# An encoder layer whose residual stream is kept as rows of tokens instead of rows of channels

## The chip, the cores and the metric

The kernel runs on one core of one Trainium2 chip. The metric is the device time of one launch in microseconds (us); the profiled execution is read beside it. Engines are named as in the profile: PE (TensorE, the matrix engine; PEld its loads of the stationary operand), DVE (VectorE), ACT (ScalarE), POOL (GpSimd) and SP (SyncE, which issues nearly all DMAs here, in order).

## The reference, cut to what matters

Two sequences (`x_prompt`, s = 0, and `x_sample`, s = 1) of 512 tokens of 1024 channels go through one layer:

```
x = x + 0.5 * swiglu(rms_norm(x, ffn1_norm), ...)          # 2816 hidden channels
h = rms_norm(x, mix_norm)
proj = h @ w_in        # queries, keys, values of attention and of the memory, gates
merged = sigmoid(g_att) * (att @ w_up_att) + sigmoid(g_mlstm) * (mem @ w_up_mlstm)
x = x + merged @ w_out
x = x + 0.5 * swiglu(rms_norm(x, ffn2_norm), ...)
y = rms_norm(x, final_norm)

def rms_norm(x, g): return x * rsqrt(mean(x * x, axis=-1) + EPS) * g
def swiglu(x, w_gate, w_up, w_down): return (silu(x @ w_gate) * (x @ w_up)) @ w_down
```

All is float32; every matrix product is made as three matmuls of high and low parts (hi x hi, hi x lo, lo x hi).

## The kernel before, in words

PE multiplies along the partitions (128 rows of the on-chip memory), so activations that enter a product as the contracted operand must have channels on the partitions. The kernel keeps the residual stream that way all along: `xbuf[s]` and `x2buf[s]` in DRAM are `[128, 8, 512]`, eight blocks of 128 channels by 512 tokens.

Stages, in order of the program:

- **Start.** `load_x` brings both inputs as token rows. For s = 0, `turn` (L1176) transposes each 128 x 128 block on PE; `keep_x` (L1181) copies the eight results out of PSUM on ACT and stores them to `xbuf[0]`. `norm_x` (DVE L1191, then the row scale, then the scaling on DVE L1199 and ACT L1197, in place) normalizes the token rows, and `turn` transposes them for ffn1 (L1218).
- **ffn1 up** (`Up.begin` for seven blocks, whose results are kept in DRAM, then `Up.rest`, a loop over 22 blocks of the hidden channels, products at L301, side work such as DVE L330 and ACT L310). The two sequences are combined in a scheme of seven products (B11, B21, B22, T4, T1, T2_, T3) instead of eight. `late_x`, called in eight rounds of the loop, transposes s = 1's input on PE (L1266) and stores it to `xbuf[1]`.
- **ffn1 down** (`ffn_down`): 28 steps, seven products for each of four chunks of hidden blocks. `products` (L545) holds weights as the stationary operand and streams 512 tokens, so PSUM gets channels by tokens. `flush_` (L562) adds half of it to the residual `xs[s]`, which was loaded from `xbuf` in four loads of 1 MB. In the last seven steps each finished 128-channel block goes to `done`: `done1` stores it, splits s = 0's for the mixer (`emit_hl`, L144 and L145), and sums squares (`sq_add`: ACT L155, POOL L156). In ffn2 the last step is done in two halves of 256 tokens.
- **The norm's scale.** A sum over channels is a sum over partitions here: `stats` transposes the sum of squares (PE L188, DVE L190), computes 1/rms (`rstd_cols`, 12 small DVE instructions, L166 to L177), and `bcast_cols` spreads it over the partitions (PE L198, DVE L204) as `R[s]`.
- **Mixer** (`mix(s, ...)`, once per sequence). It multiplies inputs that carry the gain but not yet 1/rms. The results that have tokens on the partitions (`tok_proj`, PE L695) are scaled by `r[s]` in ACT's eviction (L769 to L774); the ones with channels on the partitions (`win_cols`, PE L711) by a product with `R[s]` on DVE (L867, L876, L991, L1034). The last part works `mem_gate` and `merge_mem` for eight blocks (L1034, L1041, L1042, split into `mh`, `ml` at L613 and L614), and calls `prep1` or `prep2` for each, which prepare the next stage's input of the other sequence. Then `out_unit`, eight times, multiplies with `w_out` (PE L711, DVE L1144) into channels by tokens.
- **ffn2**, like ffn1; its begin reloads s = 1 from `x2buf[1]` and scales it (`normed`, L609).
- **Final norm.** `done2` collects the blocks; `turn_out` (L1363) transposes all of it back to token rows, 64 transposes, and `put_out` (ACT L1369, POOL L1370, DVE L1372) scales and stores.

The order of work is the program's, moved by a scheduler with priorities (`shifted`, `pin`). On chip there are seven slots of 16 KB per partition (`A(...)`: inputs, mixer tensors, residuals), four raw and four split weight buffers, and eight PSUM banks in four kinds (MM three, PO one, PS two, PT two).

Of the kernel before, what the change touches and what calls it, by code (L numbers as in the profile page):

```python
# [16 lines left out]
P = 128  # L17
# [9 lines left out]
def encoder(ctx, tc, I, outs):  # L27
# [121 lines left out]
    def sq_add(src, acc, tag="t2", qtag="f2"):  # L149
        if acc is None:  # L150
            acc = T2(F32, tag)
            nc.scalar.activation(acc, src, AF.Square)
            return acc
        q = T2(F32, qtag)
        nc.scalar.activation(q, src, AF.Square)  # L155
        nc.gpsimd.tensor_tensor(acc, acc, q, op=ALU.add)  # L156
        return acc

    def rstd_cols(v, width, n):


        def t_(dt=F32):
            return spool.tile([P, width], dt, tag=f"rs{width}", bufs=5, name=nm("rs"))
# [17 lines left out]
    def stats(acc):  # L181

        return rstd_cols(col_sums(acc), 4, D)

# [15 lines left out]

    def bcast_cols(r):
        pr = bcast_psum(r)
        R = T2(F32, "R")
        nc.vector.tensor_copy(R, pr)  # L204
        return R

# [182 lines left out]
    class Up:  # L389
# [23 lines left out]
        def rest(self, raw, late=None, at=None, hook=None):  # L413
# [12 lines left out]
            for i, j in enumerate(ORDER):  # L426
                W = left
                nxt = ORDER[i + 1] if i + 1 < NF else None
                turn_late = late(i, ring) if late else None
# [10 lines left out]
                if turn_late:  # L440
                    turn_late()
# [19 lines left out]
    def ffn_down(wd, rb, ring, tail, xres, done, at_step, hook, halves=None):  # L461
# [71 lines left out]
        def products(i, ts, ds=range(DH)):  # L533
# [3 lines left out]
            for d in ds:  # L537
                if first:
                    banks[grp, d] = (((PS, PS, PT, PT) if grp == "Y" else (MM, MM, MM, PO))[d])()
                p = banks[grp, d][:, ts]  # L540
                us = left[i]
                for q, u in enumerate(us):
                    r = right[(i + 3) % 4][q]
                    for k, (a, b) in enumerate(((0, 0), (0, 1), (1, 0))):
                        nc.tensor.matmul(p, u[:, a, d * P:(d + 1) * P], r[:, b, ts],  # L545
                                         start=(first and q == 0 and k == 0), stop=(q == len(us) - 1 and k == 2),
                                         skip_group_check=True)
                flush_(i, d, p, ts)
# [4 lines left out]
        def flush_(i, d, p, ts):  # L553
# [7 lines left out]
            else:  # L561
                V_.scalar_tensor_tensor(acc[:, ts], p, 0.5, acc[:, ts], op0=ALU.mult, op1=ALU.add)  # L562
# [8 lines left out]
            elif m == B21:  # L571
                add(xs[1][:, DH + d], e5[:, d])
                done(0, d, None)
            elif m == T4:
                done(0, DH + d, None)
            elif m == T1:
                done(1, DH + d, None)
            elif m == B22 and ts.stop - ts.start == S:
                done(1, d, None)
            elif m == B22 and d == DH - 1:  # L580
                done(1, d, ts.start * 2 // S)
# [6 lines left out]
        whole = slice(0, S)  # L588
        for s, h in ((0, 0), (1, 1), (0, 1), (1, 0)):
            nc.sync.dma_start(xs[s][:, h * DH:(h + 1) * DH, :], xres[s][:, h * DH:(h + 1) * DH, :])  # L590
        sums(CHUNKS[0])
        tail()
        for i in range(n):
            if i == n - 1 and halves:
                products(i, slice(0, S // 2))
                products(i, slice(S // 2, S))
            else:
                products(i, whole)
# [7 lines left out]

    def normed(xt, g, R, d):

        V_.scalar_tensor_tensor(xt, xt, g[:, d:d + 1], R, op0=ALU.mult, op1=ALU.mult)  # L609
# [104 lines left out]
    def mix(s, xh, xl, early=None, extra=None, after=None):  # L714
# [52 lines left out]
        def kv_done(pk):  # L767
            for b in range(4):
                nc.scalar.activation(kraw3[:, b, :], pk[b][:, 0:P], AF.Copy, scale=r[s][:, b:b + 1])  # L769
                nc.scalar.activation(Gt[:, b * 16:(b + 1) * 16], pk[b][:, 2 * P:2 * P + 16], AF.Copy,  # L770
                                     scale=r[s][:, b:b + 1])
                pv = pk[b][:, P:2 * P].rearrange("p (k e) -> p k e", k=HK)
                nc.scalar.activation(Vst[:, b, :, 0:DA], pv, AF.Copy, scale=r[s][:, b:b + 1])
                V_.scalar_tensor_tensor(Vst[:, b, :, DA:2 * DA], pv, r[s][:, b:b + 1], f(Vst[:, b, :, 0:DA]),  # L774
                                        op0=ALU.mult, op1=ALU.subtract)
# [11 lines left out]
        def q_done(pq):  # L787
            ssq = small(32, "ssq")
            for b in range(4):
                t = T2()  # L790
                nc.scalar.activation(t, pq[b], AF.Copy, scale=r[s][:, b:b + 1])
# [58 lines left out]
        def mem_values():  # L850
            def done(pvv):
                vm = A([P, 2, 4, S], F32R, "Vm")
                for b in range(4):
                    nc.scalar.activation(vm[:, 0, b, :], pvv[b], AF.Copy, scale=r[s][:, b:b + 1])
                    V_.scalar_tensor_tensor(vm[:, 1, b, :], pvv[b], r[s][:, b:b + 1], f(vm[:, 0, b, :]),
                                            op0=ALU.mult, op1=ALU.subtract)
# [16 lines left out]
        def out_gate(h):  # L873
            def done(pp):
                og = T2(F32, "ac")
                V_.tensor_tensor(og, pp, R[s], op=ALU.mult)  # L876
                nc.scalar.activation(og, og, AF.Tanh, scale=0.5)
# [16 lines left out]
        if early:  # L894
            early()
        go(*tok_proj(xh, xl, [(0, 512)], 2, q_done), mem_qk(0, 0))
        yield None
        gates()
# [99 lines left out]
        for h in range(HA):  # L998
# [5 lines left out]
            if h == 2 and extra:  # L1004
                extra()
# [25 lines left out]
        def mem_gate(d):  # L1031
            def done(pp):
                t = ths[d] = T2()
                V_.tensor_tensor(t, pp, R[s], op=ALU.mult)  # L1034
                nc.scalar.activation(t, t, AF.Tanh, scale=0.5)
# [426 lines left out]
```

## Time and profile before

| what | value |
|---|---|
| time, median of 3 runs | 2139.46 us (2139.08 to 2140.02) |
| profiled execution, span | 2143.1 us |
| PE busy | 2084.7 us (97%) |
| DVE busy | 1633.9 us (76%) |
| ACT busy | 957.6 us (45%) |
| POOL busy | 145.4 us (7%) |
| DMA | 370.23 MB, mean 173 GB/s |

The span is that of one profiled execution; its own time is the span, 3.6 us above the median of the runs. In a line of the profile, `L545 PE MATMUL pst<-rt,w 128*128 128x512 f32 x18` is a group of 18 matmuls of line 545 into a PSUM tile `pst` from `rt` and `w`, 512 columns wide; behind it, in brackets, stands how long the engine was idle ahead of it and what released it. A row of the windows gives, for a stretch from A to B: its length, the busy time and the instruction count of PE, PEld, DVE, ACT and POOL, the clock granted to PE (1.00 is full), the busy share of the DMA engines and GB/s. A row of the waits gives an engine's instruction, what it waited for, the sum of waiting, how often and the mean. A row of groups gives busy time and mean ns, then the idle time ahead and what ended it. A row of DMA issues gives the KB of each and the us from issue to landing.

### The profile page before, as it was taken

How to read it: one execution, taken by the hardware profiler on the slowest of the kernel's cores; microseconds unless marked ns; L12 is line 12 of the kernel's file. 1: busy time of each engine (PE TensorE's matmuls, PEld its weight loads, DVE VectorE, ACT ScalarE, POOL GpSimd, SP SyncE). 2: the span in 40 equal slices, each digit the busy share in tenths (PEclk: the TensorE clock that was granted, in tenths of full speed). 3: DMA queues.
4: the chain of work that ended last, by engine and by line, in shares of the span. 5: the costliest groups of instructions: out<-in, count | busy, mean ns of one | idle time of the engine just before them, and what ended most of it. 6: DMA issues, size and time to landing. Idle time of an engine off the chain costs nothing.

```text
span 2143.1 us, 27234 instructions
## 1 busy us (share of the span) xinstructions
PE 2084.7 (97%) x9544; PEld 1699.1 (79%) x9544; DVE 1633.9 (76%) x2895; ACT 957.6 (45%) x1693; POOL 145.4 (7%) x138
## 2 busy tenths in 40 slices
PE   7999999999999999999999999999999999999997
PEld 6878788887888777878887777877778788888886
DVE  7888887875797798675659967665878887776795
ACT  6534444442234456463436664434434444443222
POOL 0000000001002011100121011011000000000002
PEclk9999999999999999999999999999999999999999
DMA  9566654489765222342352233347465554389752
GB/s 293 164 206 194 214 198 151 147 305 371 275 221 164 64 76 67 92 116 73 115 167 69 69 91 104 110 148 215 153 197 172 190 190 151 123 301 384 272 190 105
DMA packets 314776, 370.23 MB, mean 173 GB/s; under 512 B 18608, under 2 KB 209088, under 8 KB 313616
## 3 DMA queue, kind: packets, MB, share of 16 engines
q1 hardware_dynamic: 314048, 367.23, 52.2%
q0 software_dynamic: 592, 1.27, 0.3%
q8 instruction: 75, 1.23, 0.2%
q14 instruction: 61, 0.50, 0.1%
HBM read 259.35 MB, written 109.08 MB: 172 GB/s over the span
## 4 chain that ended last, share of the span: by engine, by line
PE 79%; DVE 10%; DMA 6%; ACT 3%; issue 2%; SPq 0%; POOL 0%; DVEq 0%; ACTq 0%; POOLq 0%
PE mm L711 17%; PE pss L301 14%; PE pst L301 8%; PE mm L545 8%; PE mm L301 8%; PE pss L545 4%; PE pst L545 4%; PE mm L695 4%; PE pso L545 3%; DMA wr<-in_ffn_w_up_dram 2%; DMA rbuf<-t 1%; PE pso L974 1%; PE pso L695 1%; PE pst L967 1%; PE pss L948 1%
## 5 line engine op out<-in xcount | busy, mean ns | idle before, releaser
L711 PE MATMUL mm<-xh,w 128*128 128x512 f32 x896 | 290.6, 395 | 0.0
L301 PE MATMUL pss<-xc,w 128*128 128x512 f32 x1056 | 258.6, 392 | 9.2 <-DVE t L330 9.2
L301 PE MATMUL mm<-xc,w 128*128 128x512 f32 x1056 | 259.0, 394 | 5.5 <-ACT f L310 4.1
L301 PE MATMUL pst<-xc,w 128*128 128x512 f32 x1056 | 255.4, 390 | 0.0
L301 PEld LDWEIGHTS pss<-xc,w 128*128 128x128 f32 x1056 | 196.5, 188 | 56.1 <-DVE t L330 15.7
L301 PEld LDWEIGHTS mm<-xc,w 128*128 128x128 f32 x1056 | 197.6, 189 | 51.2 <-ACT f L310 7.8
L301 PEld LDWEIGHTS pst<-xc,w 128*128 128x128 f32 x1056 | 197.3, 188 | 43.2 <-ACT t L334 2.5
L711 PEld LDWEIGHTS mm<-xh,w 128*128 128x128 f32 x896 | 167.0, 188 | 32.5
L221 ACT ACTIVATE w<-wr 128x1024 fp32r<-128x1024 f32 (+1 forms) x112 | 114.6, 1029 | 166.7 <-issue 61.0
L545 PE MATMUL mm<-rt,w 128*128 128x512 f32 (+1 forms) x819 | 186.3, 383 | 1.7 <-DMA rt<-rbuf 1.7
L711 PE MATMUL mm<-xl,w 128*128 128x512 f32 x448 | 176.5, 394 | 0.0
L545 PEld LDWEIGHTS mm<-rt,w 128*128 128x128 f32 x819 | 150.2, 188 | 32.2 <-DMA rt<-rbuf 1.9
L222 DVE TENSOR_TENSOR w<-wr,w 128x1024 fp32r<-128x1024 f32 (+1 forms) x112 | 140.4, 1254 | 42.5 <-ACT w L221 41.1
L259 ACT ACTIVATE w<-t 128x512 fp32r<-128x512 f32 x176 | 107.2, 628 | 126.5 <-DVE t L285 46.8
L260 DVE TENSOR_TENSOR w<-t,w 128x512 fp32r<-128x512 f32 x176 | 118.3, 688 | 40.4 <-ACT w L259 37.4
L301 PE MATMUL pss<-xc,f 128*128 128x512 f32 x528 | 128.7, 392 | 0.2 <-DVE t L338 0.2
L301 PEld LDWEIGHTS pss<-xc,f 128*128 128x128 f32 x528 | 98.1, 188 | 24.1 <-DVE t L338 4.1
L613 ACT ACTIVATE w<-wr 128x512 fp32r<-128x512 f32 x72 | 44.7, 631 | 131.6 <-PE pso L545 63.4
L613 ACT ACTIVATE w<-t 128x512 fp32r<-128x512 f32 x82 | 51.8, 632 | 112.6 <-PE pst L545 51.6
L711 PEld LDWEIGHTS mm<-xl,w 128*128 128x128 f32 x448 | 84.2, 188 | 16.1
L545 PE MATMUL pss<-rt,w 128*128 128x512 f32 x396 | 94.3, 389 | 0.2 <-DMA rt<-rbuf 0.2
L545 PE MATMUL pst<-rt,w 128*128 128x512 f32 x396 | 93.7, 389 | 0.0
(328 smaller groups left out, 3746.2 us busy)
## 6 DMA issues: line engine op xcount, KB each, us to landing
rt<-rbuf SPq DMA_DIRECT2D x154, 512.0 KB, 5.6
wr<-in_w_in_dram SPq DMA_DIRECT2D x72, 512.0 KB, 3.9
wr<-in_ffn_w_gate_dram SPq DMA_DIRECT2D x56, 512.0 KB, 5.4
rbuf<-tab SPq DMA_DIRECT2D x90, 256.0 KB, 3.6
wr<-in_ffn_w_up_dram SPq DMA_DIRECT2D x44, 512.0 KB, 4.4
rbuf<-t SPq DMA_DIRECT2D x88, 256.0 KB, 3.6
rbuf<-f SPq DMA_DIRECT2D x66, 256.0 KB, 3.5
rbuf<-R SPq DMA_DIRECT2D x64, 256.0 KB, 3.8
```

The costliest lines, as they stand in the source:

```text
L221: pin(nc.scalar.activation(hi, raw, AF.Copy))
L222: pin(lo_eng.tensor_tensor(lo, raw, f(hi), op=ALU.subtract))
L259: pin(nc.scalar.activation(t[:, 0], src, AF.Copy))
L260: pin(V_.tensor_tensor(t[:, 1], src, f(t[:, 0]), op=ALU.subtract))
L301: nc.tensor.matmul(p, a[:, k, :], xt[:, b, k, :], start=(first and k == 0 and i == 0), stop=(k == HK_ - 1 and i == 2), skip_group_check=True)
L545: nc.tensor.matmul(p, u[:, a, d * P:(d + 1) * P], r[:, b, ts], start=(first and q == 0 and k == 0), stop=(q == len(us) - 1 and k == 2), sk ...
L613: nc.scalar.activation(hi, src, AF.Copy)
L695: nc.tensor.matmul(p[b][:, :N], a[:, k, bs], w_[:, kl, :], start=(k == 0 and i == 0), stop=(k == KD - 1 and i == 2))
L711: nc.tensor.matmul(p, a[:, k, :], b, start=(k == 0 and i == 0), stop=(k == n - 1 and i == 2))
L948: nc.tensor.matmul(p, qT[:, h, b * P:(b + 1) * P], kv[:, hk * 2 + j, :], start=(j == 0), stop=(j == 1))
L967: nc.tensor.transpose(p[:, b * P:(b + 1) * P], Ps[b][:, kb * P:(kb + 1) * P], ident)
L974: nc.tensor.matmul(po, Vst[:, kv_, hk, :], w, start=(kv_ == 0 and i == 0), stop=(kv_ == 3 and i == 1))
```

## The change

The residual stream has tokens on the partitions. `xbuf` and `x2buf` become `[128, 2, 4, 512]`: two halves of 512 channels, four blocks of 128 tokens.

- `products` exchanges the operands: 128 tokens of the activations are stationary, 512 channels of weights stream. The halves of ffn2's last step go. The residual of ffn1 is loaded straight from the inputs; `keep_x` and `late_x` go.
- `out_half`, twice for `out_unit` eight times: four PSUM banks (one per block of tokens) collect over the pairs of channel blocks; the result is added to token rows.
- Squares are summed by ACT along the row (`square`), so a row's scale (`row_scale`) needs no transposes and no broadcast; `sq_add`, `stats` and `bcast_cols` go. Rows are scaled in place (`scale_rows`) and then transposed (`turn_rows`), with the gain applied in the eviction from PSUM: `turn0` in ffn1's last down step, `prep1` and `prep2` behind the merges in the mixers (from rows fetched by `fetch_rows`), and in ffn2's begin from rows that stay on chip.
- The mixer's inputs are scaled, so all products with `r[s]` and `R[s]` go.
- The final norm scales token rows in place and stores them, without transposes.

```diff
-    def ffn_down(wd, rb, ring, tail, xres, done, at_step, hook, halves=None):
+    def ffn_down(wd, rb, ring, tail, xres, done, at_step, hook):
...
-                        nc.tensor.matmul(p, u[:, a, d * P:(d + 1) * P], r[:, b, ts],
+                        nc.tensor.matmul(p, r[:, b, d * P:(d + 1) * P], u[:, a, :],
...
-            nc.sync.dma_start(xs[s][:, h * DH:(h + 1) * DH, :], xres[s][:, h * DH:(h + 1) * DH, :])
+            nc.sync.dma_start(xs[s][:, h * DH:(h + 1) * DH, :], xres(s, h))
...
         def kv_done(pk):
             for b in range(4):
-                nc.scalar.activation(kraw3[:, b, :], pk[b][:, 0:P], AF.Copy, scale=r[s][:, b:b + 1])
+                nc.scalar.activation(kraw3[:, b, :], pk[b][:, 0:P], AF.Copy)
...
-                t = F2()
-                V_.tensor_tensor(t, pp, R[s], op=ALU.mult)
-                split(t, qks[h][:, 2 * j, :], qks[h][:, 2 * j + 1, :])
+                split(pp, qks[h][:, 2 * j, :], qks[h][:, 2 * j + 1, :])
...
-                V_.tensor_tensor(mg[:, d, :], pp, R[s], op=ALU.mult)
-                nc.scalar.activation(mg[:, d, :], mg[:, d, :], AF.Tanh, scale=0.5)
+                nc.scalar.activation(mg[:, d, :], pp, AF.Tanh, scale=0.5)
...
+        before()
         mh, ml = A([P, KD, S], F32R, "mh"), A([P, KD, S], F32R, "ml")
         go(*[mem_gate(d) for d in range(KD)])
         go(*[merge_mem(d) for d in range(KD)])
...
-        def out_unit(d):
-            def done(pp):
-                xt = T2()
-                nc.sync.dma_start(xt, xbuf[s][:, d, :])
-                V_.scalar_tensor_tensor(xt, pp, 0.5, xt, op0=ALU.mult, op1=ALU.add)
-                nc.sync.dma_start(x2buf[s][:, d, :], xt)
-                acc[0] = sq_add(xt, acc[0], "R", "t2")
-            return proj(wov[:, :, d * P:(d + 1) * P], lambda k: (mh[:, k, :], ml[:, k, :]), KD, done)
+        rows = A([P, 2, 4, S], F32, "rows") if s else None
+        def out_half(h):
+            p = []
+            def comp(k0, w):
+                if not p:
+                    p.extend([MM(), MM(), MM(), PO()])
+                for k in (k0, k0 + 1):
+                    for b in range(4):
+                        bs = slice(b * P, (b + 1) * P)
+                        for i, (a, w_) in enumerate(((mh, w[0]), (mh, w[1]), (ml, w[0]))):
+                            nc.tensor.matmul(p[b], a[:, k, bs], w_[:, k - k0, :],
+                                             start=(k == 0 and i == 0), stop=(k == KD - 1 and i == 2))
+                if k0 + 2 < KD:
+                    return
+                for b in range(4):
+                    xt = rows[:, h, b, :] if s else T2()
+                    nc.sync.dma_start(xt, xbuf[s][:, h, b, :])
+                    V_.scalar_tensor_tensor(xt, p[b], 0.5, xt, op0=ALU.mult, op1=ALU.add)
+                    nc.sync.dma_start(x2buf[s][:, h, b, :], xt)
+                    square(xt, ssq2[s][:, h, b:b + 1])
...
+    def square(x, to):
+        nc.scalar.activation(T2(F32, "f2"), x, AF.Square, accum_out=to)
+    def row_scale(sq, n=slice(0, 4)):
+        w = n.stop - n.start
+        t = spool.tile([P, 4], F32, tag="cs4", bufs=4, name=nm("rsum"))[:, 0:w]
+        V_.tensor_tensor(t, sq[:, 0, n], sq[:, 1, n], op=ALU.add)
+        return rstd_cols(t, w, D)
+    def scale_rows(rows, r):
+        for b in range(4):
+            v = rows[:, :, b, :]
+            if b % 2:
+                nc.scalar.activation(v, v, AF.Copy, scale=r[:, b:b + 1])
+            else:
+                V_.tensor_scalar(v, v, r[:, b:b + 1], None, op0=ALU.mult)
+    def turn_rows(rows, k, bank):
+        p = bank()
+        for b in range(4):
+            nc.tensor.transpose(p[:, b * P:(b + 1) * P], rows[:, k // 4, b, (k % 4) * P:(k % 4 + 1) * P], ident)
+        return p
...
-    for k in range(KD):
-        keep_x(0, k, turn(0, k, every), up.ring("x"))
     norm_x(0)
...
+    def done1(s, h, b):
+        x_ = xs[s][:, h * 4 + b, :]
+        nc.sync.dma_start(xbuf[s][:, h, b, :], x_)
+        square(x_, ssq1[s][:, h, b:b + 1])
+        if s == 0 and h == 1 and b == 3:
+            scale_rows(xs[0].rearrange("p (h b) c -> p h b c", h=2), row_scale(ssq1[0]))
+        if s == 1 and h == 0:
+            turn0(2 * b)
+            turn0(2 * b + 1)
+    def fetch_rows(buf, ssq):
+        def before():
+            t = fresh[0] = A([P, 2, 4, S], F32, "rows")
+            for h in range(2):
+                nc.sync.dma_start(t[:, h], buf[:, h])
+            scale_rows(t, row_scale(ssq))
+        return before
     def prep1(d):
...
-        xt = T2(F32, "f2")
-        nc.sync.dma_start(xt, xbuf[1][:, d, :])
-        emit_hl(xt, gm, d, *nhl[1])
+        emit_hl(turn_rows(fresh[0], d, (PS, PT)[d % 2]), gm, d, *nhl[1])
...
-        normed(x1l, g2, R2[1], k)
-        normed(x1u, g2, R2[1], k + HK_)
+        for t, kk, bank in ((x1l, k, PS), (x1u, k + HK_, PT)):
+            nc.scalar.activation(t, turn_rows(rows1, kk, bank), AF.Copy, scale=g2[:, kk:kk + 1])
...
+    def done2(s, h, b):
+        x_ = xs[s][:, h * 4 + b, :]
+        square(x_, ssq3[s][:, h, b:b + 1])
+        (V_ if (s, h) == (1, 0) else G_).tensor_tensor(x_, x_, fn[h], op=ALU.mult)
+        if s == 0 and h == 1 and b == 3:
+            n = slice(0, 4)
+        elif s == 1 and h == 0 and b % 2:
+            n = slice(b - 1, b + 1)
+        else:
+            return
+        r = row_scale(ssq3[s], n)
+        for i in range(n.start, n.stop):
+            v = xs[s].rearrange("p (h b) c -> p h b c", h=2)[:, :, i, :]
+            r_ = r[:, i - n.start:i - n.start + 1]
+            if s and i == 3:
+                V_.tensor_scalar(v, v, r_, None, op0=ALU.mult)
+            else:
+                nc.scalar.activation(v, v, AF.Copy, scale=r_)
+            nc.sync.dma_start(outs[s][0, i * P:(i + 1) * P, :].rearrange("p (h c) -> p h c", h=2), v)
```

More of the change, by code (lines that the diff above doesn't have):

```diff
@@ L199, in bcast_psum @@
         return pr
[L201 to L205, printed above, removed]
     def fetch_w(view):
@@ L411, in left, with rest @@
             return gu_left_a(self.fetch(j, (0,))[0])
-        def rest(self, raw, late=None, at=None, hook=None):
+        def rest(self, raw, at=None, hook=None):
             ring = self.ring
@@ L593, in ffn_down @@
         for i in range(n):
[L594 to L598, printed above, removed]
+            products(i)
             prep(i + 2)
```

209 lines of the change are left out of this document (51 added, 158 removed).

## The prediction

> **What bounds the kernel now.** I read the page first, for the busy shares and the chain that ended last, then the windows of single stages, then the timeline where TensorE (PE) stood still.
>
> ```profile
> span 2143.1 us, 27234 instructions
> PE 2084.7 (97%) x9544; PEld 1699.1 (79%) x9544; DVE 1633.9 (76%) x2895; ACT 957.6 (45%) x1693; POOL 145.4 (7%) x138
> PE 79%; DVE 10%; DMA 6%; ACT 3%; issue 2%; SPq 0%; POOL 0%; DVEq 0%; ACTq 0%; POOLq 0%
> ...
> 2092.45 4.24 PE L545 MATMUL pst<-rt,w 128*128 128x512 f32 x18
> 2096.53 4.24 PE L545 MATMUL pss<-rt,w 128*128 128x512 f32 x18
> ...
> 2113.30 0.60 PE L1363 MATMUL pss<-ident,xs 128*128 128x128 f32 x4
> 2113.73 0.60 PE L1363 MATMUL pst<-ident,xs 128*128 128x128 f32 x4
> ```
>
> PE is busy 97% of the span and carries 79% of the last chain, so the time is PE's instructions plus the places where PE stands. The timeline rows give its prices. Two groups of 18 matmuls of 512 columns start 4.08 us apart: 0.227 us each. Two groups of four transposes start 0.43 us apart: 0.109 us each. An instruction put on or taken off PE moves the end by these prices; work of DVE, ACT or a DMA counts only where PE waits for it. The profiled execution spans 2143.1 us, 3.6 us above the median of the runs, 2139.5; I make the sum as a difference and carry it to the median. A difference of 0.2% is 4.3 us, about the least that a measurement of this kernel tells from none.
>
> **Products.** The down products exchange the two operands: as many matmuls, 512 wide as before, so 0, except the last step of each FFN's down stage, costed with the tail. The output projection keeps 192 matmuls per sequence: 0.
>
> **Transposes.** The instruction streams have 128 new ones in the middle (32 for each sequence ahead of the mixer, 32 for each ahead of ffn2): 128 x 0.109 = +14.0. The transposes of the column sums and of the broadcasts outside the tail go, 32 of them: -3.5. `late_x` takes 32 out of ffn1's up loop. What these are worth is seen by setting that loop, with them, beside the same stretch of ffn2's, without:
>
> ```profile
> 81.50:458.80 377.30, 374.88 (x1653) 305.68 (x1653) 303.36 (x468) 162.63 (x273) 0.00 (x0) 1.00 0.57 188
> 1531.00:1908.90 377.90, 370.97 (x1620) 301.99 (x1619) 301.93 (x468) 159.97 (x264) 0.00 (x0) 1.00 0.53 177
> PE pss L301 <- DVE t L330: 9.2, 11, 1.8
> ```
>
> Both windows run from the same group of matmuls to its like: 33 more PE instructions in the first, yet 377.3 against 377.9 us. The loop is held by something else (PE's largest wait, 9.2 us for DVE at L330, lies in these loops), so I take -0.5 and keep 0 and -3.5 (32 x 0.109) as ends. Transposes together: **+10.0**, ends +7.0 and +10.5.
>
> **The tail.**
>
> ```profile
> 2112.63:2129.75 17.12, 16.41 (x136) 15.47 (x135) 11.08 (x39) 7.59 (x19) 3.84 (x3) 1.00 0.33 123
> 2129.75:2143.11 13.36, 1.09 (x9) 0.62 (x6) 6.61 (x21) 2.71 (x6) 2.53 (x2) 0.72 0.41 157
> 2132.68 0.60 ACT L1386 ACTIVATE f<-pss 128x512 f32<-128x512 f32 x1 [2.03 <-PE pss L1363]
> 2133.98 0.16 DVE L1403 TENSOR_TENSOR fs<-sq 128x2 f32<-128x2 f32 x1 [1.78 <-ACT f L1386]
> 2136.61 0.72 ACT L1369 ACTIVATE t<-t,rs 128x512 f32<-128x512 f32 x1 [2.66 <-DVE rs L177]
> 2137.95 0.74 DVE L1372 SCALAR_TENSOR_TENSOR t<-pst,rs,t 128x512 f32<-128x512 f32 x1
> ...
> 16.43 1.42 DVE L1199 TENSOR_SCALAR raw<-raw,rs 128x1024 f32<-128x1024 f32 x2 [1.67 <-PE pso L1176]
> ```
>
> From the end of the last full-width step to the end are 17.12 + 13.36 = 30.5 us. They hold 72 half-width products and the 64 transposes of the final norm. Afterwards the step is 36 x 0.227 = 8.2 us, with nothing else on PE. Behind its last matmul: the add into the residual 0.74 (as at 2137.95), the square on ACT 0.8 (0.60 and the reading of its sum), the product with the gain on DVE 0.75, which waits for the square, the row scale 2.63 (2133.98 to 2136.61), the scaling of 1024 columns 0.71 (half of the row at 16.43), and from the end of scaling to the end of the span 4.4, as now (2138.69 to 2143.11): 10.0, and 2.0 for four hand-overs of half a microsecond, an estimate. So 20.2 for 30.5: **-10.3**, ends -12 (no hand-overs) and -8 (the larger last store takes 2 us longer).
>
> **The start.** `keep_x` (32 transposes, eight copies on ACT, eight stores) goes.
>
> ```profile
> 17.29 2.19 ACT L1197 ACTIVATE raw<-raw,rs 128x1024 f32<-128x1024 f32 x2
> 14.60 0.16 DVE L177 SCALAR_TENSOR_TENSOR rs<-rs,rs 128x4 f32<-128x4 f32 x1
> 9.19:16.02 6.83, 5.20 (x25) 5.20 (x26) 3.45 (x17) 3.41 (x6) 0.43 (x1) 0.50 1.11 332
> ```
>
> The row scale is ready at 14.76, but DVE, by the row at 16.43 above, waits 1.67 us for `keep_x`'s last transposes, since it scales the same rows in place, and ACT begins at 17.29, behind its copies. Both can begin at 14.8: a gain of up to 2.5. Against it stands the clock: 0.50 from 9.19 to 16.02, and full afterwards, after 5.20 us of transposes alone. Without these PE is cold when the true transposes begin, and a half-speed window of 3.4 us costs 1.7. I take **-1.5**, ends -2.5 and +1.0. The Trainium skill ("TensorE: Matmul & The Clock Gate", Part 4: PE-mode transpose) says that transposes do not engage the full clock; the rise at 16.02 behind nothing but transposes speaks against it. By that rule the removed ones warmed nothing, the term is -2.5, and the time is 1 us lower.
>
> **Loads of ffn1's down stage.**
>
> ```profile
> xs<-xbuf SPq DMA_DIRECT2D x4, 1024.0 KB, 10.7
> ```
>
> The four 1 MB loads of the residual now read the input in pieces of 2 KB rather than 8 KB; it is the same amount in a stretch that begins with much else in the queue. I take **+1.0**, ends 0 and +1.5 (a seventh of one load).
>
> **The waits.** The inputs of the mixer are scaled before they are turned, so nothing waits for a row scale behind the products, and 56 products of DVE with the broadcast scale go, such as:
>
> ```profile
> L1034 DVE TENSOR_TENSOR t<-mm,R 128x512 f32<-128x512 f32 x16 | 11.0, 689 | 32.0 <-PE mm L711 31.9
> ...
> 688.56 0.65 PE L198 MATMUL pst<-ident,rs 128*128 128x128 f32 x4 [1.28 <-DVE rs L177]
> 690.66 0.70 PE L695 MATMUL mm<-w,xh 128*128 128x512 f32 x2 [1.45 <-DVE kv L774]
> ...
> 1028.96:1033.16 4.20, 1.41 (x10) 0.98 (x8) 3.47 (x5) 1.18 (x2) 1.26 (x1) 1.00 0.34 116
> 1033.19:1036.60 3.41, 3.41 (x18) 3.41 (x17) 1.49 (x3) 0.63 (x1) 0.00 (x0) 0.50 0.54 154
> 1429.07:1436.00 6.93, 4.33 (x11) 2.45 (x10) 6.24 (x10) 1.89 (x3) 0.00 (x0) 0.75 0.36 116
> 1473.64:1516.00 42.36, 38.90 (x164) 30.43 (x163) 34.98 (x62) 24.68 (x39) 1.72 (x1) 0.96 0.79 246
> 1511.06:1514.47 3.41, 3.41 (x9) 2.65 (x8) 1.59 (x3) 0.99 (x3) 0.00 (x0) 0.50 0.60 169
> ```
>
> - Mixer of the first sequence, keys to queries: 1.28 us for the scale, and 1.45 for a key-value eviction that stood behind it. Both go: **-2.7**, ends -2.7 and 0 (the eviction is late for another reason).
> - From the first mixer to the second: 4.20 us with 10 matmuls of 272 columns (0.12 each, as 272/512 of 0.227) is 3.0 of standing; the half-speed window behind it costs 1.7. Now a turn of 0.44 us follows each of the eight merges there, and gives DVE that much time to catch up: **-3.0**, ends -4.7 and 0.
> - Start of the last output projection: 6.93 us for 11 matmuls (2.5 at full pace) is 4.4 of standing, in wait for the last merged columns. The new order works through pairs of columns, and begins with the two merged first, so the last pair is wanted 3 x 24 matmuls, 16 us, later: **-4.0**, ends -4.4 and 0.
> - Begin of ffn2: 42.36 us for 164 instructions, of which eight are transposes: 156 x 0.227 + 8 x 0.109 = 36.3, so 6.1 of standing, 1.7 of it the half-speed window. The sums of squares on PE and the broadcast go, and the rows of the second sequence stay in the chip, so eight loads of 256 KB go; the stall on evictions whose buffers wait for stores can remain: **-3.0**, ends -6.1 and 0.
> - 56 x 0.69 = 38 us less on DVE, elsewhere beside matmuls: **-1.0**, ends -3 and 0.
>
> Together -13.7, ends -21.0 and 0.
>
> **What moves behind new waits.** In each mixer two loads of 1 MB (the rows of the other sequence) stand on SP's queue between the sixth and the seventh weight block of the memory gates; ACT and DVE wait for them in order, and the splits of blocks seven and eight stand behind. The cover is the work from gate three to six, 4 x 24 x 0.227 = 21.8 us, against 10.7 for each load on a crowded queue: 0, and if the cover is gone, a wait of some microseconds twice. The first sequence's turns stand in ffn1's last down step, between its products; its rows are complete two steps of 8.2 us before, and scaling (four of 0.7 to 1.1 us, on two engines) and the scale's 2.63 fit in: 0.
>
> **The sum.** +10.0 - 10.3 - 1.5 + 1.0 - 13.7 = -14.5, so 2139.5 - 14.5 = **2125**. With all good ends: 7.0 - 12 - 2.5 + 0 - 21.0 = -28.5, 2111. With all bad ends: 10.5 - 8 + 1 + 1.5 + 0 = +5, 2144.5.
>
> **The rivals.**
>
> *The waits stay (0.08).* Each of the four standing places has another cause close behind the named one: evictions, weight splits, the half clock. Then +10.0 - 10.3 - 1.5 + 1.0 = -0.8: 2138.7. For it: three of them come with a half-speed window, which can fall elsewhere. Against it: the waits named in the rows are for things that no longer exist.
>
> *Everything goes (0.10).* All good ends, **2111**; for it speaks that PE gets slack from DVE in every merge.
>
> *Turns stall PE (0.09).* Each of the 32 turns stands in PE's one queue, and everything behind waits if its bank is not yet evicted or its rows not yet scaled.
>
> ```profile
> L144 ACT ACTIVATE xh<-f,gain 128x512 fp32r<-128x512 f32 x8 | 5.3, 713 | 2.3 <-DMA f<-xbuf 2.3
> L145 DVE SCALAR_TENSOR_TENSOR xl<-f,gain,xh 128x512 fp32r<-128x512 f32 x8 | 7.0, 885 | 0.0
> L188 PE MATMUL pst<-ident,R 128*128 128x128 f32 x4 | 0.7, 286 | 0.9 <-POOL R L156 0.9
> ```
>
> A turn's bank is held for 0.71 + 0.89 = 1.6 us by ACT and DVE, and both are in order behind other work. At 1 us of wait each the sum is -14.5 + 32 = +17.5: **2157**, slower. It decides from 14.5 / 32 = 0.45 us a turn. Against it: four banks take turns, and 12 matmuls (2.7 us) lie between two turns in the merges.
>
> *A transpose costs its whole length (0.03).* The last row above has 286 ns for one, where the spacing in a run of them is 109. If a turn between matmuls paid the length, the 96 transposes more would cost 96 x (0.286 - 0.109) = 17 above my term: 2142. The spacing of the rows at the top speaks against it. The Trainium skill (the same page and section) states about 275 ns for one in a kernel's context, which agrees with the length, not the spacing.
>
> **How the numbers follow.** My forecast has 0.70, with 2116 to 2133 as its own range, all of it faster by over 0.2%. Faster: 0.70 + 0.10 = 0.80. Same: 0.07 of the staying waits and 0.02 of the dear transposes, 0.09. Slower: 0.09 of stalling turns and 0.02 of the rest, 0.11. The range goes from 2111 to 2140: it takes in the staying waits and the good ends, and leaves out the stalling turns and the worst corner.
>
> **What would show it.** In the profile of the changed kernel: last full-width product to the end about 20 us; no wait of PE for a row scale in the mixers; the places at 1030, 1430 and 1475 to 1515 without a half-speed window; 128 transposes 0.11 us apart, with no wait ahead of them; the up loops unchanged at 377 us. I am wrong if PE's waits name the turned banks, the scaled rows or their loads, or if the standing places keep their length.

## The result, and the profile after

| kernel | median us | range | against before, 95% interval |
|---|---|---|---|
| before | 2139.74 | 2139.08 to 2143.63 | |
| changed | 2130.45 | 2128.64 to 2131.81 | 0.9954 [0.994, 0.9968] |

By the medians the change made the kernel 9.3 us faster (0.43%; the ratio of the runs is 0.9954, and by its interval the gain is 0.3% to 0.6%). Forecast were 14.5 us, 2125, with a range from 2111 to 2140. The page of the changed kernel, its first lines and the chain that ended last:

```profile
span 2130.0 us, 26826 instructions
PE 2071.1 (97%) x9472; PEld 1689.2 (79%) x9472; DVE 1579.5 (74%) x2817; ACT 968.5 (45%) x1739; POOL 104.1 (5%) x110
PE 74%; DVE 10%; DMA 6%; issue 6%; ACT 4%; POOL 0%; SPq 0%; DVEq 0%; ACTq 0%; POOLq 0%
```

PE is the bound as before. DVE lost 54 us of work; what most of that was worth is tested below.

The windows of the changed kernel at the places of the prediction (columns as before: length, busy time and count of PE, PEld, DVE, ACT, POOL, then the clock):

```profile
674.81:708.78 33.97, 33.97 (x196) 30.18 (x195) 18.95 (x45) 16.21 (x34) 1.33 (x10) 1.00 0.47 132
1026.00:1038.00 12.00, 12.00 (x89) 11.43 (x87) 8.54 (x11) 5.32 (x7) 0.85 (x1) 1.00 0.39 123
1424.00:1437.00 13.00, 12.04 (x54) 9.63 (x53) 6.54 (x9) 5.00 (x7) 0.00 (x0) 1.00 0.93 306
1468.81:1511.00 42.19, 41.53 (x194) 32.89 (x193) 31.84 (x59) 33.04 (x56) 0.00 (x0) 1.00 0.62 201
2106.85:2115.40 8.55, 8.55 (x38) 6.76 (x36) 3.44 (x5) 6.34 (x14) 4.24 (x3) 1.00 0.65 245
2115.40:2130.00 14.60, 0.01 (x1) 0.00 (x0) 7.56 (x32) 4.78 (x7) 0.00 (x0) 0.63 0.38 144
```

Keys to queries (first row), the change of mixers (second) and ffn2's begin (fourth) run without a half-speed window, and PE hardly stands; at the last output projection (third) it stands 1.0 us. The last two rows are the last step and the tail: the step is 8.5 us (forecast 8.2), the tail 14.6 instead of the 12.0 that were added up.

The main waits of PE in the changed kernel (the sum, how often, the longest single one):

```profile
PE pss L1147 <- DVE raw L1195: 13.7, 2, 11.3
PE pss L282 <- DVE t L311: 12.4, 14, 2.3
PE pst L848 <- DVE t L581: 4.4, 4, 1.8
PE pss L906 <- ACT t L911: 3.5, 3, 2.0
PE mm L282 <- ACT f L291: 2.4, 5, 0.8
PE pst L185 <- DVE rs L168: 1.7, 4, 0.5
PE mm L1106 <- DVE t L995: 1.0, 1, 1.0
```

The first is the start: 11.3 us until the first rows are scaled, 2.4 for the second sequence's. The mixers' waits for a row scale and for key-value evictions are gone (L185 is the scale of the memory's heads, which both kernels have). The up loops' wait (L311, L330 before) has not become smaller: 12.4 us, against 9.2 before. No wait names a turn (L1177).

### The profile page after: what moved, and what is told of

It is laid out like the page before. It is cut to its first block, busy times and chain, and to the rows that moved or that the text cites. A ratio compares the mean times of both kernels' runs of the same rounds, so it can differ in the third digit from the quotient of the medians.

```text
span 2130.0 us, 26826 instructions
## 1 busy us (share of the span) xinstructions
PE 2071.1 (97%) x9472; PEld 1689.2 (79%) x9472; DVE 1579.5 (74%) x2817; ACT 968.5 (45%) x1739; POOL 104.1 (5%) x110
## 4 chain that ended last, share of the span: by engine, by line
PE 74%; DVE 10%; DMA 6%; issue 6%; ACT 4%; POOL 0%; SPq 0%; DVEq 0%; ACTq 0%; POOLq 0%
PE mm L678 14%; PE pss L282 13%; PE pst L282 8%; PE mm L523 8%; PE mm L282 7%; PE pss L523 4%; PE pst L523 4%; PE mm L662 3%; PE pso L523 3%; DMA rbuf<-t 2%; DMA wr<-in_ffn_w_up_dram 2%; PE pso L932 1%; PE mm L1106 1%; PE pso L1062 1%; DVE w L241 1%
## 5 line engine op out<-in xcount | busy, mean ns | idle before, releaser
L282 PE MATMUL pss<-xc,w 128*128 128x512 f32 x1056 | 258.4, 391 | 12.4 <-DVE t L311 12.4
L203 DVE TENSOR_TENSOR w<-wr,w 128x1024 fp32r<-128x1024 f32 (+1 forms) x112 | 135.9, 1215 | 106.0 <-ACT w L202 100.7
L523 PE MATMUL mm<-w,rt 128*128 128x512 f32 x792 | 185.6, 390 | 1.1 <-DMA rt<-rbuf 1.1
L523 PEld LDWEIGHTS mm<-w,rt 128*128 128x128 f32 x792 | 148.4, 188 | 32.5 <-DMA rt<-rbuf 1.8
L523 PE MATMUL pss<-w,rt 128*128 128x512 f32 x396 | 94.0, 389 | 0.0
L523 PE MATMUL pst<-w,rt 128*128 128x512 f32 x396 | 93.7, 389 | 0.0
```

Source lines behind the costliest of these rows:

```text
L203: pin(lo_eng.tensor_tensor(lo, raw, f(hi), op=ALU.subtract))
L282: nc.tensor.matmul(p, a[:, k, :], xt[:, b, k, :], start=(first and k == 0 and i == 0), stop=(k == HK_ - 1 and i == 2), skip_group_check=True)
L523: nc.tensor.matmul(p, r[:, b, d * P:(d + 1) * P], u[:, a, :], start=(first and q == 0 and k == 0), stop=(q == len(us) - 1 and k == 2), ski ...
```

## Experiments

### The kernel before, profiled again

> The kernel before, profiled once more, unchanged. The two spans so far differ by 13.1 us (2143.1 and 2130.0), the medians by 9.3. Theory: the first profile of before was a long execution, and a second one has a span of about 2138 to 2140, with the missing 3 to 4 us spread over stages that wait for DMAs (the up loops, the start of the down stages). Rival: the span is again about 2143 and the profiled execution is simply longer than the timed ones; then the 13.1 us by stages stand as they are.

```profile
span 2139.7 us, 27234 instructions
...
1473.43:1516.00 42.57, 39.49 (x172) 30.78 (x171) 37.09 (x66) 25.80 (x41) 1.72 (x1) 1.00 0.77 248
...
PE mm L301 <- ACT f L310: 1.9, 3, 1.0
```

The theory held for the span: it is 2139.7 (2141.47 timed), 3.4 us shorter than the first. Most of the difference is in ffn2's begin and up loop (433.5 instead of 437.9 us); the other stages differ both ways. The half-speed window at 1511 isn't there, the clock is 1.00, and the wait for ACT's evictions there is 1.9 us, with 1.0 the longest, instead of 2.6 and 1.8. That window belonged to one execution, not to the kernel. The second profile has others instead: the granted clock is 0.50 from 688.3 to 691.7, and at 1030 for 6.8 us instead of 3.4. This gives two columns of before. A stage begins with PE's first matmul in it, read from the timeline. "Spread" is what the changed kernel and all variants below that leave a stage alone took for it, one profile each; "forecast" is the sum of the prediction's terms that lie in the stage.

| stage, until | before (1st, 2nd profile) | changed | spread | forecast of the difference |
|---|---|---|---|---|
| start and ffn1 up, to the first down product | 461.6, 460.5 | 460.5 | 459.4 to 463.2 | -2.0 |
| ffn1 down, to the first mixer | 212.3, 210.5 | 214.3 | 212.9 to 216.7 | +4.5 |
| keys to queries | 38.7, 40.3 | 34.0 | 33.9 to 34.0 | -3.6 |
| to the first attention product | 24.5, 24.5 | 25.7 | 24.3 to 26.4 | 0 |
| to the second mixer | 291.7, 290.8 | 294.9 | 293.2 to 294.9 | +3.0 |
| its keys, queries, first output projection | 105.6, 108.5 | 103.4 | 103.0 to 103.4 | -3.9 |
| to ffn2 | 339.3, 338.3 | 336.1 | 336.1 to 337.6 | -1.9 |
| ffn2's begin and up loop | 437.9, 433.5 | 436.8 | 432.8 to 438.0 | -0.4 |
| ffn2 down and tail, to the end | 231.5, 232.7 | 224.4 | 224.2 to 225.8 | -10.3 |

What differs by less than its spread says nothing: about 5 us in ffn2's begin and up loop, and nearly 4 in the first two stages.

### More work on PE at the start

```diff
-    for _ in range(8):
+    for _ in range(52):
         pin(nc.tensor.matmul(pw, ones, ones, start=True, stop=True))
```

> The changed kernel with 52 matmuls of ones at the start instead of 8, so that TensorE works until the first rows are scaled. In the changed kernel the first 16 true transposes were 0.213 us apart (16.12 to 19.68 us), then 0.109. Theory (the removed copies of x had kept the clock up): the first transposes stand 0.109 apart, and the first product of ffn1 starts 1.0 to 1.7 us earlier than at 21.03; time 1 to 1.7 us shorter than the changed kernel's. Rival (the start is paced by ScalarE's and VectorE's evictions and weight splits): the transposes are faster, but the first ten products end where they did (within 0.5 us), time the same. Second rival (transposes run at half speed whatever went before): still 0.213 apart.

The timeline of the changed kernel, with some of its transposes (four in 1.06 us, then eight in 1.16), and its first product:

```profile
15.22 2.19 ACT L1193 ACTIVATE raw<-raw,rs 128x1024 f32<-128x1024 f32 x2 [13.01 <-DVE rs L168]
17.97 1.06 PE L1147 MATMUL pss<-ident,raw 128*128 128x128 f32 x4
19.68 1.16 PE L1147 MATMUL mm<-ident,raw 128*128 128x128 f32 x8
21.03 2.55 PE L282 MATMUL mm<-xc,w 128*128 128x512 f32 x10
```

and with 52 matmuls of ones:

```profile
11.80 3.74 PE L1127 MATMUL pst<-ones 128*128 128x128 f32 x32
17.07 0.60 PE L1147 MATMUL pst<-ident,raw 128*128 128x128 f32 x4
17.50 0.60 PE L1147 MATMUL pss<-ident,raw 128*128 128x128 f32 x4
19.60 2.79 PE L282 MATMUL mm<-xc,w 128*128 128x512 f32 x11
```

The transposes run at full pace (four in 0.60 us) and the first product comes 1.4 us earlier, as the theory has it. That the slow pace is the clock's is seen in the run with the gain on DVE (below), whose start is the same and whose record of the clock reaches back further than that of the changed kernel, which starts at 19.92 (two windows, then two rows of the timeline):

```profile
8.49:18.72 10.23, 3.14 (x15) 2.91 (x16) 6.38 (x24) 4.05 (x5) 0.23 (x1) 0.50 1.08 319
18.73:37.00 18.27, 14.07 (x71) 10.93 (x70) 16.70 (x44) 13.16 (x23) 0.00 (x0) 1.00 0.89 282
...
17.43 1.06 PE L1147 MATMUL pss<-ident,raw 128*128 128x128 f32 x4
18.94 1.04 PE L1147 MATMUL mm<-ident,raw 128*128 128x128 f32 x8
```

Up to 18.7 the clock is 0.50 and four transposes take 1.06 us, behind it eight take 1.04.

What the earlier product is worth at the end, these runs can't tell. The time is 2129.39 us, 1.1 less than the changed kernel's, with ranges that overlap (2125.86 to 2130.60 against 2128.64 to 2131.81). The first down product starts at 460.26, against 460.47, but over nine profiles with the same start and loop it lies anywhere from 459.4 to 463.2. Some 0.5 us is lost at once, when PE waits for the second sequence's rows, 2.9 us for 2.4.

### Transposes back in ffn1's up loop

```diff
+                if extra and 3 <= i < 19 and i % 2:
+                    extra()
...
+    def extra():
+        p = PO()
+        for b in range(4):
+            nc.tensor.transpose(p[:, b * P:(b + 1) * P], ident, ident)
```

> The changed kernel with 32 transposes of the identity put into eight rounds of ffn1's up loop, where the kernel before had those of late_x (without its copies and DMAs). Theory (the loop's end is set by something else than TensorE's sum: the first down product of ffn1 began between 460.3 and 461.6 us in six profiles, although the first product of ffn1 began at 19.6 in one and at 21 in the others): the first down product starts within 0.8 us of that. Rival (TensorE is the bound there): 3.5 us later.

The first down product starts at 461.12, amid the 459.4 to 463.2 of the others, and the time is 2128.47 (2128.27 to 2128.59), no longer than the changed kernel's: no cost is seen where the rival had 3.5 us. So the 32 transposes of `late_x` were nearly free before, and removing them bought nothing that these runs could see. For those of `keep_x`, which stood ahead of the loop, no run shows it.

### Each turn made twice

```diff
         p = bank()
-        for b in range(4):
+        for b in (0, 1, 2, 3, 0, 1, 2, 3):
             nc.tensor.transpose(p[:, b * P:(b + 1) * P], rows[...], ident)
```

> The changed kernel with every turn of scaled rows made twice into the same bank (128 more transposes: 32 in the last step of ffn1's down stage, 32 in each mixer's merges, 32 in ffn2's begin). Theory (a transpose costs its spacing on TensorE, 0.109 us, and nothing else waits): 128 x 0.109 = 14.0 us longer than the changed kernel, 3.5 in each of the four stages. Rival (some of the turns stand in time in which TensorE waits for VectorE anyway, as in the merges): 2 us or less in the stage of the merges. Second rival (a transpose costs its length, some 0.28): 36 us.

2141.46 us, 11.0 above the changed kernel (against before 1.0005 [0.9994, 1.0016]; with the interval of the changed kernel, the 11 can be 7 to 15). Against the mean of the changed kernel and the variants that leave a stage alone: the down stage +2.6, the first mixer +3.1, the second +2.7, ffn2's begin and up +1.7 (the first and the last are within those stages' own spread), 10.1 together. So 10 to 11 us over 128, 0.08 to 0.09 us for a transpose: these runs can't tell it from its spacing of 0.109 (14 us), but it is far from its length (36). In the merges little slack takes it up.

### VectorE's products put back

```diff
-                split(pp, qks[h][:, 2 * j, :], qks[h][:, 2 * j + 1, :])
+                t = F2()
+                times_one(t, pp)
+                split(t, qks[h][:, 2 * j, :], qks[h][:, 2 * j + 1, :])
...
-                nc.scalar.activation(og, pp, AF.Tanh, scale=0.5)
+                times_one(og, pp)
+                nc.scalar.activation(og, og, AF.Tanh, scale=0.5)
```

and so in both other gates; `times_one` multiplies by ones.

> The changed kernel with the 56 products of VectorE in the evictions of the mixers put back, as products with ones (128 x 512 from PSUM; nothing waits for a scale, so only their time comes back). Theory (they lay beside matmuls): both mixers together 1 us longer, 3 at the most. Rival (VectorE is close to setting the pace of the mixers, at 0.69 us x 56 = 38 us of its time): 4 us or more.

2129.77 us, no longer than the changed kernel (2130.45). By stages: the first mixer 292.7 for 294.9, the second 339.7 for 336.1, together +1.4. One wait of the second mixer grew:

```profile
PE pss L913 <- ACT t L918: 3.7, 1, 3.7
```

from 2.0 (L906 and L911 of the changed kernel). So 38 us of DVE's work were worth little, 1 us by the stages and nothing by the times; both are well short of the rival's 4.

### What took the standing at the last output projection away

Three runs: the pairs of merged columns taken from the last to the first; the gain of `prep2` on DVE, which the kernel before had there; and both.

```diff
-                    for k0 in range(0, KD, 2)]
+                    for k0 in range(KD - 2, -1, -2)]
```

```diff
-        nc.scalar.activation(xt, p, AF.Copy, scale=g2[:, d:d + 1])
+        V_.tensor_scalar(xt, p, g2[:, d:d + 1], None, op0=ALU.mult)
```

> The changed kernel, its output projection working through the pairs of merged columns from the last to the first, instead of from the first to the last. Theory (the 4.4 us of standing at 1429 to 1436 in the kernel before went because the last merged columns are now wanted 16 us later): TensorE stands again at the start of the second sequence's output projection, 3 to 5 us between the last transposes of the merges and full pace, with the half-speed window or without; the first sequence's output projection, which lies behind other products, is not changed; time 3 to 5 us longer. Rival (the standing went because the turns between the merges give VectorE time): less than 1 us of it comes back.

> The changed kernel, the gain in prep2's eviction (eight blocks of 128 x 512 from PSUM, behind the merges of the second mixer) on VectorE instead of ScalarE, which gives VectorE 0.74 us more in each merge, as it had in the kernel before. The order of the output projection was shown not to be what took the standing of 4.4 us away at its start. Theory (it went because VectorE lost one 0.74 us operation a merge and TensorE got 0.44 us more): TensorE stands 3 to 5 us at the start of the output projection again. Rival (the turns alone give enough room: a merge has 3.16 us of TensorE against 2.0 to 2.8 us of VectorE): below 1.5 us, as now 1.0.

> The changed kernel with both of the former edits: the output projection from the last pair of columns to the first, and prep2's gain on VectorE. Either alone brought the standing at the start of the second sequence's output projection to 1.0 and 1.9 us, of 4.4 in the kernel before. Theory (either the order or VectorE's room is enough by itself): together 3 to 5 us of standing. Rival (the 0.44 us turn on TensorE behind each merge alone keeps VectorE abreast): 2 us or less also together.

PE's waits around the start of that projection, with the order reversed:

```profile
PE mm L1106 <- ACT mh L580: 1.0, 1, 1.0
```

with the gain on DVE:

```profile
PE mm L1106 <- DVE t L995: 1.9, 2, 1.0
```

with both, and the window there:

```profile
PE mm L1106 <- ACT mh L580: 4.6, 1, 4.6
...
1424.00:1436.00 12.00, 9.65 (x35) 7.81 (x36) 7.29 (x11) 4.42 (x6) 0.00 (x0) 0.86 0.84 264
```

Neither edit alone brings the standing back; both bring 4.6 us of it, and the clock falls with it (0.86 over 12 us). The stage takes 342.4 us instead of 336.1 to 337.8. So there are two reasons of which one is enough: DVE is less far behind at the end of the merges, and the last columns are wanted later. The prediction named the second alone. But 4.6 us is not the old 4.4 rebuilt. The reversed order wants the last pair at once, while the kernel before came to its last two columns after 18 matmuls (4 us), so DVE was further behind there than in the run of both. The times (2129.56, 2131.59, and a single 2135.5) don't decide: the second run's own executions reach 2136.12. The stage and the waits do.

### The tail

The timeline of the changed kernel near its end:

```profile
2105.74 4.28 ACT L1352 ACTIVATE xs<-xs,rs 128x1024 f32<-128x1024 f32 x4 [1.90 <-DVE rs L168]
2110.70 2.54 POOL L1338 TENSOR_TENSOR xs<-xs,tab 128x512 f32<-128x512 f32 x2 [5.47 <-ACT f L1152]
2112.49 1.29 DVE L1338 TENSOR_TENSOR xs<-xs,tab 128x512 f32<-128x512 f32 x1 [2.48 <-ACT f L1152]
2113.20 2.20 PE L523 MATMUL pso<-w,rt 128*128 128x512 f32 x9
2118.26 0.69 DVE L540 SCALAR_TENSOR_TENSOR xs<-pso,xs 128x512 f32<-128x512 f32 x1
2119.04 0.63 ACT L1152 ACTIVATE f<-xs 128x512 f32<-128x512 f32 x1 [1.62 <-DVE rs L166]
2122.84 0.16 DVE L168 SCALAR_TENSOR_TENSOR rs<-rs,rs 128x2 f32<-128x2 f32 x1
2123.10 1.15 ACT L1352 ACTIVATE xs<-xs,rs 128x1024 f32<-128x1024 f32 x1 [1.02 <-DVE rs L168]
2123.11 0.75 DVE L1350 TENSOR_SCALAR xs<-xs,rs 128x1024 f32<-128x1024 f32 x1
```

PE's last matmul ends at 2115.4; DVE adds its block (L540) only at 2118.26. Three ways to shorten this:

```diff
# GpSimd takes three of the last four products with the gain
-        (V_ if (s, h) == (1, 0) else G_).tensor_tensor(x_, x_, fn[h], op=ALU.mult)
+        (V_ if (s, h, b) == (1, 0, 3) else G_).tensor_tensor(x_, x_, fn[h], op=ALU.mult)
```

> The changed kernel, the final norm's products with the gain of three of the last four blocks on GpSimd instead of VectorE (only the last one stays). In the changed kernel the last matmul ends near 2115.3, but VectorE adds the last block to the residual only at 2118.26, and from the last matmul to the end are 14.7 us. Theory (VectorE's queue is late by 2.9 us, since in it each product waits for ScalarE's square, and 13 small instructions stand between): the last addition comes within 1 us of the last matmul, and the end 1.5 to 2.5 us earlier. Rival (the stores set the end): the chain on VectorE is earlier, the end moves by less than 0.5 us. Second rival: GpSimd's products (1.3 to 1.5 us each) are late themselves and the end is later by 1 us or more.

```profile
2109.71 6.26 POOL L1338 TENSOR_TENSOR xs<-xs,tab 128x512 f32<-128x512 f32 x5 [5.47 <-ACT f L1152]
2110.37 0.69 DVE L540 SCALAR_TENSOR_TENSOR xs<-mm,xs 128x512 f32<-128x512 f32 x1 [1.35 <-PE mm L523]
2112.31 1.22 DVE L157 TENSOR_SCALAR rs<-rsum 128x2 f32<-128x2 f32 x1
2119.08 0.68 DVE L540 SCALAR_TENSOR_TENSOR xs<-pso,xs 128x512 f32<-128x512 f32 x1
```

The second rival: the last matmul starts at 2114.0, DVE's last addition even later behind it, and from that start to the end are 17.8 us, 2.8 more than the changed kernel's 15.0. GpSimd works without a break for 6.3 us. Small instructions of DVE stand ahead of the last addition, and the three from 2112.31 on take 1.2 us each, for 0.17 elsewhere. The time is 2132.09 us, 0.9968 [0.9958, 0.9978] of before.

```diff
# VectorE takes two of the first sequence's four scalings
-            if s and i == 3:
+            if (s and i == 3) or (not s and i % 2):
                 V_.tensor_scalar(v, v, r_, None, op0=ALU.mult)
```

> The changed kernel, of the four scalings of the first sequence's finished rows in the last step two on VectorE, instead of all four on ScalarE. In the changed kernel ScalarE scales from 2105.7 to 2110.0, and the squares of the second sequence's blocks, GpSimd's products behind them and VectorE's products, which run 1.29 instead of 0.69 us while GpSimd works, all come late. Theory (the queue on ScalarE starts the delay): the last addition to the residual comes 1 to 2.5 us earlier against the last matmul, and the end too. Rival (VectorE has no room for 1.5 us more there): no change, or up to 1.5 us later.

```profile
2104.89 2.19 ACT L1352 ACTIVATE xs<-xs,rs 128x1024 f32<-128x1024 f32 x2 [1.90 <-DVE rs L168]
2112.35 2.20 PE L523 MATMUL pso<-w,rt 128*128 128x512 f32 x9
2115.35 0.68 DVE L540 SCALAR_TENSOR_TENSOR xs<-pso,xs 128x512 f32<-128x512 f32 x1
```

The last addition comes 0.8 us behind the last matmul's end instead of 2.9, and the end 2.1 us earlier (12.9 us from the start of the last matmul). The theory held: four scalings on ACT had held up the squares, then GpSimd's products, then DVE's. 2127.57 us, 0.9936 [0.9921, 0.9951] of before.

```diff
# besides, scale and gain of the last four blocks in one operation at the end
-        (V_ if (s, h) == (1, 0) else G_).tensor_tensor(x_, x_, fn[h], op=ALU.mult)
+        if (s, h) != (1, 0):
+            G_.tensor_tensor(x_, x_, fn[h], op=ALU.mult)
...
+            if s:
+                V_.scalar_tensor_tensor(v[:, 0], v[:, 0], r_, fn[0], op0=ALU.mult, op1=ALU.mult)
+                nc.scalar.activation(v[:, 1], v[:, 1], AF.Copy, scale=r_)
```

> As the last one (two of the first sequence's four scalings on VectorE), and besides the second sequence's last four blocks are not multiplied by the gain beforehand: scale and gain are applied together at the end on VectorE (0.75 us a block), ScalarE scales the other halves (0.65). So no VectorE instruction in the last step waits for a square until the last sum. Theory (VectorE's waits for the squares, 2.5 us ahead of the first product with the gain, and the products themselves, are the rest of its delay): from the last matmul to the end 1 to 2 us less than the 12.9 us of the last one, 11 to 12. Rival (the end is set by four stores of 512 KB, which move for some 1.3 us each, behind the chain): less than 0.5 us.

From the last matmul to the end 12.1 us: 0.8 less, between the two expectations. 2127.66 us, 0.9949 [0.9936, 0.9961]: by the times no different from the one before it. Either beats the kernel before clearly. By the medians both lie some 3 us under the changed kernel too, with ranges that overlap its own (2125.84 to 2128.98 against 2128.64 to 2131.81); 2.1 and 2.9 us is what their tails show.

## Why the prediction was right, and where its size was off

**Direction and mechanism.** PE's added transposes are paid for by waits that go and by the tail. The measured 9.3 us lie in the range; that is a third less than the 14.5 in the sum. The terms that were too good are the start and the tail, with 1.1 us that came back in the first mixer.

**Base.** The sum was made against a long execution. A run's time is not its span but some 1.8 us more (2131.81 and 2130.0 for the changed kernel, 2141.47 and 2139.7 for the second profile of before), so the first profile, with a span of 2143.1, lay some 5 us above the median of the runs, not 3.6. The 1.7 for the half-speed window at 1511 and part of the wait ahead of it were costs of that execution. From the second profile of before the standing of ffn2's begin is 42.57 - 164 x 0.227 - 8 x 0.109 = 4.5 us, not 6.1; afterwards it is 42.19 - 162 x 0.227 - 32 x 0.109 = 1.9. So 2.6 were gained where 3.0 were forecast, and the up loop behind varies by more.

**Transposes, +10.0.** The price of the spacing is borne out as far as the runs can tell: 11 us, with 7 to 15 possible, for 14.0 by the spacing. Taking -0.5 rather than -3.5 for `late_x` was right in its reason; the run shows no cost. The stages that got turns grew as forecast or somewhat less: ffn1 down by 2.0 to 3.8 (forecast +4.5, with 1.0 of it for the loads of the residual, which no wait of PE names), the first mixer by 3.2 to 4.1 (+3.0).

**The start, -1.5: nothing of it is seen.** Both halves of the working came true. The scalings begin together, at 15.22 (forecast 14.8; the row scale itself came 0.4 us later). And the transposes pay for a cold clock: they are 0.213 us apart until 19.89, 17 x 0.104 = 1.8 us. The two cancel: the first product came at 21.03, before at 21.05 and 21.36. In the profiles with the same start it lies from 20.2 to 21.9, by when the clock rises (18.7 to 21.9). Whether a warm clock would gain anything in the end stays open: the row of the up loops that was read for `late_x` makes one expect that the loop takes it back, but the one run for it can't show so small a gain. The full pace from 19.9 came after transposes alone, a second time. The Trainium skill ("TensorE: Matmul & The Clock Gate", Part 4: PE-mode transpose) has it that they do not engage the full clock; the trace disagrees.

**The tail, -10.3: too large by 2 to 3.** It measured -7.1 and -8.3 against the two profiles of before: step and tail took 8.5 + 14.6 = 23.1 us for the 20.2 of the forecast. The last step's 8.5 us were nearly right (8.2). The chain behind it was added up from durations, on the assumption that DVE, ACT and GpSimd come to it with empty queues. They did not: ACT was still scaling the other sequence, and all in-order queues behind inherited that, so DVE's last addition came 2.9 us behind the last matmul. Moving two instructions gave 2.1 of it back. From that addition to the end are 11.7 us, close to the 12.0 that were added up, but by luck. The 2.0 for four hand-overs of half a microsecond is shown by no run: the square on ACT starts 0.1 us behind the addition, the scaling 0.1 us behind the row scale. In its place the scaling on ACT took 1.15 us instead of 0.71, and from its end to the end of the span are 5.8 us instead of 4.4.

**Keys to queries, -3.6 with the transposes of the scale in it: -4.7 and -6.3.** PE runs through it without a gap. The larger figure has the half-speed window at 688 in it, which the first profile hasn't. But 1.1 us came back up to the first attention product (25.7 for 24.5; 24.3 to 26.4 in the variants), where PE waits for DVE's splits: it seems that a wait moved, in part, behind the removed one.

**From the first mixer to the second, -3.0, and the last output projection, -4.0.** The stages show -2.3 to -5.1 with -0.9 of transposes in the forecast, and -2.2 to -3.2 with turns in it (forecast -1.9): right in size. The reason given for the second was only one of two, as the three runs show. For the first no such runs were made; that the turns give DVE its time there is argued, not shown.

**The rivals.** The waits stay: the named ones went. The half clock did fall elsewhere, though. The changed kernel's own profile has no half-speed window between 41 us and the tail, but of the ten variants' profiles five have one at 723 to 730 and six at 1136 to 1146, 1.7 us for each 3.4. Turns that stall PE: none of PE's waits names one, and doubling them cost no more than their spacing. The dear transpose: refuted by the same run. The loads of rows between the weight blocks: no wait of PE names them.

## What to carry to other kernels

A loop that does not get longer when work is put into it will not get shorter when work is taken out: decide first which stages pass a gain on to the end, and set the others to zero. Before reading a gain of 1 or 2 us out of a stage, see how far that stage strays over kernels that leave it alone. A chain behind the last matmul is not the sum of its durations; read from the in-order queues what is still in front of it on each engine. And where two edits each remove a standing place, undoing one alone shows nothing; undo both.

## What the runs showed of the hardware beside that

Some VectorE instructions don't end before a GpSimd product beside them does. In the changed kernel a small instruction took 1.16 us in place of 0.17, and ended at 2102.02, with GpSimd's product (2101.99); a product took 1.29 in place of 0.69 (2112.49 above):

```profile
2100.71 1.28 POOL L1338 TENSOR_TENSOR xs<-xs,tab 128x512 f32<-128x512 f32 x1 [0.50 <-ACT f L1152]
2100.86 1.16 DVE L157 TENSOR_SCALAR rs<-rsum 128x4 f32<-128x4 f32 x1
2102.06 0.17 DVE L159 TENSOR_SCALAR rs<-rs 128x4 int32<-128x4 int32 x1
```

Not all do: the addition at 2110.37 of the run with GpSimd's products, which reads one operand from PSUM, took its usual 0.69 us beside one. In that run three small instructions took 1.2 us each, each ending with a product: work moved from VectorE to GpSimd came back as waiting on VectorE.
